# Group softmax on one core: twelve tiles computed in place, stores and loads issued in bursts of six on one DMA ring

## The chip, the cores and the metric

The kernel runs on one core of one Trainium2 chip. The metric is the device time of one execution in microseconds (us); the median of several runs is compared. The engines that matter here are VectorE (DVE in the rows), ScalarE (ACT) and SyncE (SP), which issues all the transfers; 16 DMA engines carry these out. TensorE does nothing, and GpSimd (POOL) only writes four constants.

## The reference

```python
def reference(x):                       # x: 4 x 4096 x 4352, float32
    B, N, D = x.shape
    G = 8
    Dg = D // G                         # 544
    x_g = x.reshape(B, N, G, Dg)
    x_g = x_g - x_g.max(axis=-1, keepdims=True)
    exp = np.exp(x_g)
    out = exp / exp.sum(axis=-1, keepdims=True)
    return out.reshape(B, N, D)
```

Each of the 16,384 rows has 8 groups of 544 numbers, and each group gets its own softmax. The input is read once and the output, which is as large, is written once.

## The kernel before

The rows are cut into 128 tiles of 128 rows (one row for each partition of SBUF); a tile is 128 x 4352 float32, 17,408 bytes in each partition and 2,228,224 bytes in all (2176 KB). For each tile:

- SP issues the load of `xt` (L32).
- VectorE takes the negated maximum of the eight groups into `mx` in one instruction (L35).
- ScalarE computes the exponentials of `xt` into a second tile `ot`, one group at a time, with `mx` as the bias; each of the eight instructions also leaves the sum of its group in `sm` (L40).
- VectorE takes the reciprocals `rs` of the eight sums (L49) and multiplies `ot` by them in place, one group at a time (L51).
- SP issues the store of `ot` (L52).

`xt` and `ot` have four buffers each, eight tiles in all. All 256 transfers go through SP's one queue, and SP issues them in order: where an instruction of SP waits, everything behind it in its list waits too. The framework puts in the semaphores, and it chose the order of the instructions on each engine, which is not that of the loop: in the trace four loads go out together behind one store, and three more stores follow them, in a cycle of four tiles.

Of the kernel before, what the change touches and what calls it, by code (L numbers as in the profile page):

```python
# [1 line left out]

# [4 lines left out]


@with_exitstack
def kernel(  # L10
    ctx: ExitStack,
    tc: tile.TileContext,
    x: bass.AP,
    out: bass.AP,
):
    nc = tc.nc
    G = 8
    P = 128
    xf = x.flatten_outer_dims()
    of = out.flatten_outer_dims()  # L20
    N, D = xf.shape
    Dg = D // G
    xg = xf.rearrange("n (g d) -> n g d", g=G)
    og = of.rearrange("n (g d) -> n g d", g=G)
    ntiles = N // P

    pool = ctx.enter_context(tc.tile_pool(name="io", bufs=4))
    small = ctx.enter_context(tc.tile_pool(name="small", bufs=4))

    for t in range(ntiles):  # L30
        xt = pool.tile([P, G, Dg], mybir.dt.float32)
        nc.sync.dma_start(out=xt, in_=xg[t * P:(t + 1) * P])  # L32

        mx = small.tile([P, G], mybir.dt.float32)
        nc.vector.reduce_max(out=mx, in_=xt, axis=mybir.AxisListType.X, negate=True)  # L35

        sm = small.tile([P, G], mybir.dt.float32)
        ot = pool.tile([P, G, Dg], mybir.dt.float32)
        for g in range(G):
            nc.scalar.activation(  # L40
                out=ot[:, g, :],
                in_=xt[:, g, :],
                func=mybir.ActivationFunctionType.Exp,
                bias=mx[:, g:g + 1],
                scale=1.0,
                accum_out=sm[:, g:g + 1],
            )
        rs = small.tile([P, G], mybir.dt.float32)
        nc.vector.reciprocal(out=rs, in_=sm)  # L49
        for g in range(G):  # L50
            nc.vector.tensor_scalar_mul(out=ot[:, g, :], in0=ot[:, g, :], scalar1=rs[:, g:g + 1])  # L51
        nc.sync.dma_start(out=og[t * P:(t + 1) * P], in_=ot)  # L52


# [1 line left out]
_INS = ['x']  # L56
_OUTS = [((4, 4096, 4352), 'float32')]


# [23 lines left out]
```

## Time and profile before

| what | value |
|---|---|
| median of 3 runs | 1601.17 us (1600.88 to 1601.21) |
| span of the profiled execution, first to last instruction | 1599.5 us |
| median less that span | 1.7 us |
| VectorE busy | 1048.2 us |
| ScalarE busy | 760.8 us |
| bytes moved by SP's queue | 570.44 MB |
| share of the 16 DMA engines' span that its packets took | 85.6% |

The profiled execution's own time is its span and what lies around it; the 1.7 us between the median and the span stands for the latter. Busy shares are averages over the span. The share of the DMA engines counts the time of each packet, and can exceed 1 in a short stretch where packets overlap. Times in the rows are us from the span's start unless they are marked ns.

### The profile page before, as it was taken

What the parts mean: (1) busy time and instruction counts of PE and PEld (TensorE: products, weight loads), DVE (VectorE), ACT (ScalarE), POOL (GpSimd) and SP (SyncE); (2) the same over time, 40 slices, a digit from 0 to 9 for tenths busy, and PEclk for the clock granted to TensorE, in tenths of its full rate; (3) what the DMA queues carried; (4) which work ended last, traced back from release to release, by engine and by line L of the source; (5) the groups of instructions that cost most, each with busy time, mean ns of one, the idle gap of its engine ahead of it and who ended that gap; (6) DMA issues with size and microseconds to landing.
All of it is one profiled execution on the core that took longest, in us unless ns stands there. A gap on an engine that the chain in (4) does not pass through costs nothing.

```text
span 1599.5 us, 4255 instructions
## 1 busy us (share of the span) xinstructions
DVE 1048.2 (66%) x1280; ACT 760.8 (48%) x2049; POOL 0.2 (0%) x4
## 2 busy tenths in 40 slices
DVE  7568655587556775567765677656776567765566
ACT  6245444455444554445544355443554435544354
POOL 0000000000000000000000000000000000000000
DMA  8888998888988889888898888998889988898887
GB/s 362 355 341 349 376 383 346 337 349 369 390 348 341 349 355 390 361 337 353 351 383 369 341 349 355 374 378 336 344 359 376 376 342 341 362 375 371 344 340 312
DMA packets 36897, 570.71 MB, mean 357 GB/s; under 512 B 4096, under 2 KB 4096, under 8 KB 4096
## 3 DMA queue, kind: packets, MB, share of 16 engines
q1 hardware_dynamic: 36864, 570.44, 85.6%
q14 instruction: 33, 0.27, 0.0%
HBM read 285.21 MB, written 285.21 MB: 357 GB/s over the span
## 4 chain that ended last, share of the span: by engine, by line
DMA 33%; DVE 27%; ACT 26%; issue 10%; SPq 1%; DVEq 0%; ACTq 0%
DMA xt<-in_x_dram 33%; ACT ot L40 26%; DVE ot L51 18%; DVE mx L35 8%; DVE rs L49 1%; SPq L32 1%; SPq L52 1%; DVEq L78 0%; ACTq L78 0%
## 5 line engine op out<-in xcount | busy, mean ns | idle before, releaser
L40 ACT ACTIVATE ot<-xt,mx 128x544 f32<-128x544 f32 x1024 | 750.7, 734 | 817.8 <-DVE mx L35 667.3
L35 DVE TENSOR_REDUCE mx<-xt 128x8 f32<-128x4352 f32 x128 | 599.5, 4683 | 426.0 <-DMA xt<-in_x_dram 426.0
L51 DVE TENSOR_SCALAR ot<-ot,rs 128x544 f32<-128x544 f32 x1024 | 434.3, 499 | 4.5
L40 ACT ACTIVATION_READ_ACCUMULATOR ot<-xt,mx 128x1 f32 x1024 | 191.4, 187 | 0.0
L49 DVE RECIPROCAL rs<-sm 128x8 f32<-128x8 f32 x128 | 25.5, 199 | 113.3 <-ACT ot L40 113.3
L40 ACT ACT_TABLE_LOAD x1 | 1.3, 1283 | 9.7 <-DMA xt<-in_x_dram 9.7
L67 POOL MEMSET const-uint8-127<- 128x1 uint8 x1 | 0.1, 102 | 0.0
L67 POOL MEMSET const-bfloat16-1.0<- 128x1 bf16 x1 | 0.1, 101 | 0.0
L67 POOL MEMSET const-float32-0.0<- 128x1 f32 x1 | 0.1, 98 | 0.2 <-issue 0.2
L67 POOL MEMSET const-float32-1.0<- 128x1 f32 x1 | 0.1, 98 | 0.0
## 6 DMA issues: line engine op xcount, KB each, us to landing
xt<-in_x_dram SPq DMA_DIRECT2D x128, 2176.0 KB, 17.1
out_dram<-ot SPq DMA_DIRECT2D x128, 2176.0 KB, 6.6
```

The source lines that it names most:

```text
L32: nc.sync.dma_start(out=xt, in_=xg[t * P:(t + 1) * P])
L35: nc.vector.reduce_max(out=mx, in_=xt, axis=mybir.AxisListType.X, negate=True)
L40: nc.scalar.activation(out=ot[:, g, :], in_=xt[:, g, :], func=mybir.ActivationFunctionType.Exp, bias=mx[:, g:g + 1], scale=1.0, accum_out= ...
L49: nc.vector.reciprocal(out=rs, in_=sm)
L51: nc.vector.tensor_scalar_mul(out=ot[:, g, :], in0=ot[:, g, :], scalar1=rs[:, g:g + 1])
L52: nc.sync.dma_start(out=og[t * P:(t + 1) * P], in_=ot)
L67: nc = _bacc.Bacc("TRN2", target_bir_lowering=False, num_devices=1)
```

## The change

A tile now has one buffer instead of two: ScalarE writes the exponentials over `xt`, VectorE scales them there, and the store reads the same buffer. The pool has twelve buffers instead of eight. The instructions of each engine run in the order in which the program writes them (`manual_schedule`). VectorE's order is the maximum of tile i, then the reciprocals and the scaling of tile i-1. SP's order is twelve loads, then six stores, six loads, six stores, and so on. Load i+12 writes the buffer of tile i, and so it has to wait until store i has landed. Behind the first twelve there are 20 bursts of loads: 19 of six, and one of two. All transfers still go through SP's one queue, and the number and shapes of the instructions on VectorE and ScalarE are the same.

```diff
+    NBUF = 12
...
-    pool = ctx.enter_context(tc.tile_pool(name="io", bufs=4))
+    pool = ctx.enter_context(tc.tile_pool(name="io", bufs=NBUF))
...
-    for t in range(ntiles):
-        xt = pool.tile([P, G, Dg], mybir.dt.float32)
-        nc.sync.dma_start(out=xt, in_=xg[t * P:(t + 1) * P])
+    def load(i):
+        xt = pool.tile([P, G, Dg], f32, name="xt")
+        tiles[i] = xt
+        nc.sync.dma_start(out=xt, in_=xg[i * P:(i + 1) * P])
 
-        mx = small.tile([P, G], mybir.dt.float32)
+    def store(i, eng):
+        eng.dma_start(out=og[i * P:(i + 1) * P], in_=tiles.pop(i))
+
+    def expo(i):
+        xt = tiles[i]
+        mx = small.tile([P, G], f32, name="mx")
         nc.vector.reduce_max(out=mx, in_=xt, axis=mybir.AxisListType.X, negate=True)
-
-        sm = small.tile([P, G], mybir.dt.float32)
-        ot = pool.tile([P, G, Dg], mybir.dt.float32)
+        sm = small.tile([P, G], f32, name="sm")
+        sums[i] = sm
         for g in range(G):
             nc.scalar.activation(
-                out=ot[:, g, :],
+                out=xt[:, g, :],
                 in_=xt[:, g, :],
...
-        rs = small.tile([P, G], mybir.dt.float32)
-        nc.vector.reciprocal(out=rs, in_=sm)
+    def scale(i):
+        xt = tiles[i]
+        rs = small.tile([P, G], f32, name="rs")
+        nc.vector.reciprocal(out=rs, in_=sums.pop(i))
         for g in range(G):
-            nc.vector.tensor_scalar_mul(out=ot[:, g, :], in0=ot[:, g, :], scalar1=rs[:, g:g + 1])
-        nc.sync.dma_start(out=og[t * P:(t + 1) * P], in_=ot)
+            nc.vector.tensor_scalar_mul(out=xt[:, g, :], in0=xt[:, g, :], scalar1=rs[:, g:g + 1])
...
+    B = NBUF // 2
+    with tc.manual_schedule():
+        for i in range(NBUF):
+            load(i)
+        for i in range(nt + 1):
+            if i < nt:
+                expo(i)
+            if i:
+                scale(i - 1)
+                store(i - 1, nc.sync)
+                if i % B == 0:
+                    for j in range(i - B + NBUF, min(i + NBUF, nt)):
+                        load(j)
```

## Rows read from the trace of the kernel before

**Rows 1.** The page: span, busy time of each engine, transfers and their queue

```profile
span 1599.5 us, 4255 instructions
...
DVE 1048.2 (66%) x1280; ACT 760.8 (48%) x2049; POOL 0.2 (0%) x4
...
DMA packets 36897, 570.71 MB, mean 357 GB/s; under 512 B 4096, under 2 KB 4096, under 8 KB 4096
...
q1 hardware_dynamic: 36864, 570.44, 85.6%
```

**Rows 2.** Waits: us in total, times, longest; the engines, whole span

```profile
ACT ot L40 <- DVE mx L35: 667.3, 33, 21.6
DVE mx L35 <- DMA xt<-in_x_dram: 426.0, 64, 13.2
```

**Rows 3.** Waits of SP's own queue, whole span, same columns

```profile
SPq L52 <- DVE ot L51: 1397.0, 127, 24.1
```

**Rows 4.** SP's timeline, two stretches, merged: start, us until the last one's end, count

```profile
0.73 2.80 SPq L32 DMA_DIRECT2D xt<-in_x_dram  x4
...
85.73 22.77 SPq L52 DMA_DIRECT2D out_dram<-ot  x4
108.59 3.96 SPq L32 DMA_DIRECT2D xt<-in_x_dram  x4
```

**Rows 5.** Windows of one cycle: stretch, us, busy (x), clock, DMA share, GB/s

```profile
85.73:91.96 6.23, 6.19 (x6) 3.74 (x11) 0.00 (x0) 1.00 0.85 359
91.96:94.70 2.74, 2.74 (x6) 2.74 (x8) 0.00 (x0) 1.00 0.00 0
94.70:100.08 5.38, 5.34 (x6) 3.21 (x11) 0.00 (x0) 1.00 0.98 414
100.08:102.84 2.76, 1.89 (x5) 2.76 (x9) 0.00 (x0) 1.00 0.01 6
...
108.19:108.97 0.78, 0.00 (x0) 0.00 (x0) 0.00 (x0) 1.00 0.00 0
108.97:115.41 6.44, 0.00 (x0) 0.00 (x0) 0.00 (x0) 1.00 1.04 384
```

**Rows 6.** Windows in which transfers stand back to back, same columns

```profile
37.46:53.26 15.80, 10.85 (x17) 7.46 (x22) 0.00 (x0) 1.00 0.99 422
4.00:22.00 18.00, 10.94 (x7) 8.88 (x22) 0.00 (x0) 1.00 1.00 428
108.97:136.19 27.22, 13.71 (x12) 10.37 (x29) 0.00 (x0) 1.00 0.99 410
```

**Rows 7.** VectorE's timeline, first reduction and one cycle: start, us, idle before

```profile
9.69 4.68 DVE L35 TENSOR_REDUCE mx<-xt 128x8 f32<-128x4352 f32 x1 [9.69 <-DMA xt<-in_x_dram]
...
121.05 4.69 DVE L35 TENSOR_REDUCE mx<-xt 128x8 f32<-128x4352 f32 x1 [12.91 <-DMA xt<-in_x_dram]
126.24 4.69 DVE L35 TENSOR_REDUCE mx<-xt 128x8 f32<-128x4352 f32 x1 [0.51 <-DMA xt<-in_x_dram]
...
135.36 4.68 DVE L35 TENSOR_REDUCE mx<-xt 128x8 f32<-128x4352 f32 x1
...
143.49 4.68 DVE L35 TENSOR_REDUCE mx<-xt 128x8 f32<-128x4352 f32 x1
```

**Rows 8.** The page's costliest groups: busy, mean ns, idle before and releaser

```profile
L40 ACT ACTIVATE ot<-xt,mx 128x544 f32<-128x544 f32 x1024 | 750.7, 734 | 817.8 <-DVE mx L35 667.3
L35 DVE TENSOR_REDUCE mx<-xt 128x8 f32<-128x4352 f32 x128 | 599.5, 4683 | 426.0 <-DMA xt<-in_x_dram 426.0
L51 DVE TENSOR_SCALAR ot<-ot,rs 128x544 f32<-128x544 f32 x1024 | 434.3, 499 | 4.5
```

**Rows 9.** The store's instructions: ns min, median, max; first and last start

```profile
L52 SPq DMA_DIRECT2D out_dram<-ot x128: 332/343/348, 24.1 to 1592.1; - x128
```

**Rows 10.** The page's DMA issues: count, KB each, median us to landing

```profile
xt<-in_x_dram SPq DMA_DIRECT2D x128, 2176.0 KB, 17.1
out_dram<-ot SPq DMA_DIRECT2D x128, 2176.0 KB, 6.6
```

More of the change, by code (lines that the diff above doesn't have):

```diff
@@ L24 @@
     og = of.rearrange("n (g d) -> n g d", g=G)
-    ntiles = N // P
-    pool = ctx.enter_context(tc.tile_pool(name="io", bufs=4))
+    nt = N // P
+    pool = ctx.enter_context(tc.tile_pool(name="io", bufs=NBUF))
     small = ctx.enter_context(tc.tile_pool(name="small", bufs=4))
-    for t in range(ntiles):
-        xt = pool.tile([P, G, Dg], mybir.dt.float32)
-        nc.sync.dma_start(out=xt, in_=xg[t * P:(t + 1) * P])
-        mx = small.tile([P, G], mybir.dt.float32)
+    f32 = mybir.dt.float32
+    tiles = {}
+    sums = {}
+    def load(i):
[7 more added lines that the diff above has]
+        mx = small.tile([P, G], f32, name="mx")
         nc.vector.reduce_max(out=mx, in_=xt, axis=mybir.AxisListType.X, negate=True)
-        sm = small.tile([P, G], mybir.dt.float32)
-        ot = pool.tile([P, G, Dg], mybir.dt.float32)
+        sm = small.tile([P, G], f32, name="sm")
+        sums[i] = sm
         for g in range(G):
             nc.scalar.activation(
-                out=ot[:, g, :],
+                out=xt[:, g, :],
                 in_=xt[:, g, :],
```

## The prediction

> **What bounds the kernel now.** I read the page's totals first. No compute engine fills the span: VectorE is busy for 1048.2 us of 1599.5, ScalarE for 760.8, and the packets of SP's queue for 85.6% of the 16 DMA engines' time [rows 1]. So the transfers are nearest to being the bound, but they too have some 14% over, about 230 us, and the question is who leaves the DMA engines empty, and whether they could go faster when they are not.
>
> The waits answer the first half. ScalarE waits 667.3 us for the maximum, VectorE 426.0 us in 64 waits for loads [rows 2]; and SP, from which the loads must come, stood 1397.0 us in 127 waits for the scaling that a store needs [rows 3]. That is a circle: compute waits for a load, the load stands behind a store in SP's list, the store waits for compute. SP's timeline shows it: four stores at VectorE's pace within 22.77 us, and only behind the last of them four loads in one go [rows 4]. The windows of that cycle show the price: nothing moves for 2.74, 2.76 and 0.78 us, always between one store's end and the next one's start [rows 5]. At these places the engines are not slow, they have nothing queued. VectorE in turn stands idle for 12.91 us, because all four tiles are used up when the loads start [rows 7].
>
> The second half is the rate while something is queued. Loads alone run at 428 GB/s in an 18 us window, and three stores in a row at 422 GB/s, with a DMA share of 1.00 and 0.99 [rows 6]. The mean of 357 GB/s [rows 1] is thus a full rate with holes in it.
>
> **The change, part by part.** The number and shapes of the compute instructions stay, so their busy time stays as in [rows 8], and no byte is saved. What changes is when transfers are queued.
>
> *In place.* VectorE's scaling is in place already, at 499 ns an instruction [rows 8]. For ScalarE writing over what it reads the trace has no row. The bounds: nothing, or the instruction twice as long. ScalarE needs 8 x 0.734 = 5.9 us a tile, and two transfers of a tile take over 10 us (below), so even 11.7 us would only just bind; I take nothing, since the same engine reads and writes as much as before. What hides compute altogether is the transfers: 10.4 us a tile against VectorE's 8.13 us, the distance from one reduction to the next in an undisturbed stretch (143.49 - 135.36) [rows 7].
>
> *Twelve buffers and bursts of six.* Is anything ever missing in the ring? I go through SP's new list. The twelve loads land by 9.69 + 11 x 5.2 = 67 us. Store 0 can be issued at about 24.1 us, as before [rows 9], and store k some 8.13k us later, store 5 at 65 us; the ring gets to them from 67 us on, one every 5.2 us, so all are ready. Load 12 waits for store 0 to land (72 us), load 17 for store 5 (about 99 us); when SP stands at that last wait, loads 12 to 16 are still in the ring, 26 us of work. Stores 6 to 11 stand behind load 17 in SP's list; their data are ready between 73 and 114 us, and the ring reaches them from 130 us on. From then on a cycle of six tiles takes the ring some 63.5 us and VectorE 6 x 8.13 = 48.8 us, so compute catches up with the loads and then follows each as it lands. The added wait is that scaling of tile i-1 stands behind the maximum of tile i on VectorE, and so behind load i. The worst case is the last tile of a burst, whose scaling needs the first load of the next burst; but in the ring that load comes ahead of all six stores of which this is the last, by about 50 us. Issuing costs SP about 1 us a load (3.96 us for four [rows 4]) against 5.2 us of transfer. So I find no hole after the start. At the end the last loads stand ahead of the last eight stores, 42 us, in which two tiles are computed.
>
> *What a transfer costs in a full ring.* A single store takes 5.38 us from its first to its last packet; three back to back take 15.80 us, so each further one costs (15.80 - 5.38) / 2 = 5.21 us [rows 5, 6]. A store with loads right behind it takes 6.44 us instead of 5.38 [rows 5]; this switch from store to load, 1.06 us, is paid once a cycle before and after. From its start to the end of the four loads are 27.22 us, so a load costs (27.22 - 6.44) / 4 = 5.20 us [rows 5, 6]. A switch from load to store shows no price: the store issued at 85.73 us, while the last load was still moving, ended 6.23 us after its issue, and one issued to idle engines lands after 6.6 us [rows 5, 10]. Its bounds are nothing and another 1.06 us; I take nothing.
>
> **The sum.** First load landed at 9.69 us [rows 7]; 127 further loads, 127 x 5.20 = 660.4; 128 stores, 128 x 5.21 = 666.9; 20 switches (20 bursts of loads behind stores), 20 x 1.06 = 21.2; and the end. The last store is issued at 1592.1 of 1599.5 [rows 1, 9], 7.4 us before the end, of which 6.2 are its start and data, so 1.2 us lie behind the data. Together 1359.4 us of span, and with the 1.7 us by which the median exceeds the span, 1361 us: 15% less than 1601.17.
>
> **A rule that speaks against it.** The mean of the whole span is 357 GB/s [rows 1]. The Trainium skill, "DMA: Bandwidth & Descriptors", section "Where 436 GB/s comes from", says that transfers between HBM and SBUF are bound by HBM at about 358 GB/s for a core. By that the kernel stands at its limit already; by the rows it does not, as windows of 14 to 18 us run at 422 to 428 GB/s and the holes hold no packets [rows 5, 6]. The skill's "HBM Reference", section "Specifications (TRN2)", itself adds that a core streaming alone gets well above that share, about 425 GB/s, which is what these rows show.
>
> **The rivals.**
>
> *A ceiling on long stretches.* The rates above come from stretches under 30 us, each with a hole near it. If memory gave 357 GB/s over any longer time, 570.44 MB would need 1598 us, and with start and end about 1600 to 1605: no change. For it speaks only that the mean is near a round share; against it, that each hole ends when compute releases a store [rows 3].
>
> *Slower because reads and writes disturb each other all the time.* Before, loads and stores stand in the ring together only about one store in four, and there the store takes 6.44 us [rows 5]. After, both kinds are queued nearly always. If every transfer then cost 6.44 us, 256 x 6.44 = 1649 us, with 9 us of start, end and surroundings about 1658 us: slower by 3.5%. It decides from a mean of (1601 - 9) / 256 = 6.2 us a transfer. Against it: the four loads behind that store pay nothing, though all are queued at once.
>
> *A lower sustained rate.* If back-to-back transfers fell to the 5.38 us of a single store, 256 x 5.38 = 1377, plus 21.2 and 7 for start, end and surroundings: 1406 us.
>
> *The ring runs dry once a cycle*, say at the wait of the sixth load for the sixth store, by a hole like those of 2.74 us [rows 5]: 20 x 2.74 = 55 us, 1416 us; several such holes, up to 1590. Against it stand the 26 us in the ring at that moment.
>
> *The switch costs less or more.* If it is free in long bursts, 1340 us; if load to store costs 1.06 us as well, 1382 us.
>
> **Numbers.** The full ring, with the switch at any of its bounds (1338 to 1383): 0.78. Less than that: 0.02. The lower sustained rate (1384 to 1410): 0.08. A dry ring (to 1590): 0.06. The ceiling: 0.03. Slower through disturbance: 0.03. The range 1338 to 1400 us takes in the first and most of the lower rate, and leaves out under 2 in 10. A difference of 0.2% is about what a measurement of this kernel can tell from none: faster 0.94, within it 0.03, slower 0.03.
>
> **What would show it.** Right: SP's queue has packets for over 95% of the span, windows of 50 us in its middle show 410 to 425 GB/s, and no window of 2 us is empty between the start and the end; VectorE's only large wait is for loads, about 300 us in all (1359 less 1048); SP's waits are for landed stores rather than for the scaling. Wrong: empty windows at each change of bursts (dry ring), a share near 1 at 360 GB/s (ceiling or disturbance, which differ in whether stores or all packets are longer), ScalarE's exponentials well over 734 ns (in place), or VectorE busy without a break.

## The result, and the profile after

The changed kernel takes 1342.9 us (median of 4 runs, 1342.61 to 1343.89) against 1601.15 us: a ratio of 0.8389, 95% interval 0.8377 to 0.8401, faster by 16.1%. 1361 us was forecast, 1338 to 1400 as the range. The direction and the mechanism were right, the time lies 18 us under the forecast.

The page of the changed kernel answers to [rows 1], [rows 8] and [rows 10]; its line numbers are those of the new code (L45 maximum, L49 exponentials, L63 scaling, L37 load, L40 store):

```profile
span 1342.1 us, 4119 instructions
...
DVE 1038.4 (77%) x1280; ACT 764.4 (57%) x2049; POOL 0.2 (0%) x4
...
GB/s 400 427 430 427 432 430 432 427 431 429 431 429 430 431 431 430 431 431 430 431 430 431 430 431 431 430 430 431 431 431 430 430 431 429 431 430 432 431 430 258
...
q1 hardware_dynamic: 36864, 570.44, 99.4%
...
L49 ACT ACTIVATE xt<-xt,mx 128x544 f32<-128x544 f32 x1024 | 751.3, 735 | 539.5 <-DVE mx L45 295.5
L45 DVE TENSOR_REDUCE mx<-xt 128x8 f32<-128x4352 f32 x128 | 599.0, 4679 | 270.7 <-DMA xt<-in_x_dram 270.7
...
xt<-in_x_dram SPq DMA_DIRECT2D x128, 2176.0 KB, 31.1
out_dram<-xt SPq DMA_DIRECT2D x128, 2176.0 KB, 41.3
```

The compute engines work as long as before, on a shorter span: 1038.4 and 764.4 us. The same 570.44 MB fill 99.4% of the DMA engines' time where they filled 85.6%, and the rate is 427 to 432 GB/s in all slices but the first and the last; the last falls to 258.

SP's own waits answer to [rows 3] (us in total, times, longest):

```profile
SPq L37 <- DMA out_dram<-xt: 715.4, 116, 15.1
SPq L40 <- DMA xt<-in_x_dram: 371.7, 81, 5.8
SPq L37 <- DMA xt<-in_x_dram: 66.0, 14, 5.0
SPq L40 <- DVE xt L63: 42.3, 6, 13.4
```

The 1397.0 us of waiting for the scaling are down to 42.3. What SP now waits for is landed transfers, loads too, which the program's data would not ask for. The ring holds the transfers that have been issued and have not landed. The stores' median from issue to landing says how many these are when a store goes out: 41.3 us is eight transfers of 5.17 us (below). SP never has more than eight in flight in this trace; the ninth load goes out at 9.35 us, when the first has landed. That wait was not foreseen, and it costs nothing, because seven are left in the ring.

The windows of the middle and of the end answer to [rows 6]; columns as there, the DMA share is the last but one:

```profile
100.00:1300.00 1200.00, 935.09 (x1154) 686.53 (x1843) 0.00 (x0) 1.00 1.01 430
600.00:650.00 50.00, 43.72 (x51) 29.82 (x80) 0.00 (x0) 1.00 1.00 429
1000.00:1050.00 50.00, 35.73 (x44) 24.97 (x67) 0.00 (x0) 1.00 1.01 433
...
1322.00:1324.00 2.00, 0.00 (x0) 0.00 (x0) 0.00 (x0) 1.00 1.01 435
1326.00:1334.00 8.00, 0.00 (x0) 0.00 (x0) 0.00 (x0) 1.00 0.26 111
1336.00:1340.00 4.00, 0.00 (x0) 0.00 (x0) 0.00 (x0) 1.00 0.12 52
```

At 431 GB/s, the mean of the two windows of 50 us, a transfer of 2,228,224 bytes takes 2.228 / 0.431 = 5.17 us. The end shows something new: from 1326 us on the share is 0.26 and then 0.12, that is four and then two of the 16 DMA engines. Twelve are done at about 1326 us, and the last two work 15 us longer.

This does not arise at the end. A transfer lands in 16 parts, and the trace keeps the time of each. The last part came 1.8 us after the first for a transfer that landed at 114 us, 10.0 us after it at 675 us and 15.6 us at the end; at 345 us four parts were already 3.0 to 5.8 us behind. So the lag builds up over the whole span, by about 1%. Which engines these are, and why they are slower, the trace does not show.

### The profile page after: what moved, and what is told of

Read it like the earlier page. It is cut to its first block, busy times and chain, and to the rows that moved or that the text cites. A ratio compares the mean times of both kernels' runs of the same rounds, so it can differ in the third digit from the quotient of the medians.

```text
span 1342.1 us, 4119 instructions
## 1 busy us (share of the span) xinstructions
DVE 1038.4 (77%) x1280; ACT 764.4 (57%) x2049; POOL 0.2 (0%) x4
## 3 DMA queue, kind: packets, MB, share of 16 engines
q1 hardware_dynamic: 36864, 570.44, 99.4%
## 4 chain that ended last, share of the span: by engine, by line
DMA 92%; DVE 4%; ACT 1%; issue 1%; SPq 0%; DVEq 0%; ACTq 0%
DMA out_dram<-xt 61%; DMA xt<-in_x_dram 31%; DVE mx L45 2%; DVE xt L63 2%; ACT xt L49 1%; SPq L40 0%; SPq L37 0%; DVE rs L61 0%; DVEq L105 0%; ACTq L105 0%
## 5 line engine op out<-in xcount | busy, mean ns | idle before, releaser
L49 ACT ACTIVATE xt<-xt,mx 128x544 f32<-128x544 f32 x1024 | 751.3, 735 | 539.5 <-DVE mx L45 295.5
L45 DVE TENSOR_REDUCE mx<-xt 128x8 f32<-128x4352 f32 x128 | 599.0, 4679 | 270.7 <-DMA xt<-in_x_dram 270.7
L63 DVE TENSOR_SCALAR xt<-xt,rs 128x544 f32<-128x544 f32 x1024 | 434.2, 498 | 4.5
L49 ACT ACTIVATION_READ_ACCUMULATOR xt<-xt,mx 128x1 f32 x1024 | 191.5, 187 | 0.0
## 6 DMA issues: line engine op xcount, KB each, us to landing
out_dram<-xt SPq DMA_DIRECT2D x128, 2176.0 KB, 41.3
```

The source lines that it names most:

```text
L49: nc.scalar.activation(out=xt[:, g, :], in_=xt[:, g, :], func=mybir.ActivationFunctionType.Exp, bias=mx[:, g:g + 1], scale=1.0, accum_out= ...
L63: nc.vector.tensor_scalar_mul(out=xt[:, g, :], in0=xt[:, g, :], scalar1=rs[:, g:g + 1])
```

## The experiments

Two questions were put: which part of the change the gain comes from, and what became of the 1.06 us that a change from store to load was to cost. All times below are medians; ratios are to the kernel before, run on the same chip.

**alt1: one store and one load in turn.**

```diff
-    B = NBUF // 2
+    B = 1
+    AHEAD = 7
+    nxt = NBUF
...
-                    for j in range(i - B + NBUF, min(i + NBUF, nt)):
-                        load(j)
+                    while nxt < min(i + AHEAD, nt):
+                        load(nxt)
+                        nxt += 1
```

> The changed kernel with one store and one load in turn instead of bursts of six (loads run six to seven tiles ahead of the stores): 116 changes from store to load instead of 20, and the ring as full as before. In the changed kernel 12 of the 16 DMA engines end at about 1325.5 us and four end 15 us later. Theory A, each change from store to load costs a few of the engines about 0.77 us (15.4 / 20), and the slowest sets the end: 1343 + 96 x 0.77 = about 1417 us. Rival B, those four engines are simply slower per byte, whatever the order: no change, 1343 us. Rival C, the price of the prediction, 1.06 us on all engines for each change: 1343 + 96 x 1.06 = about 1445 us.

1342.42 us, ratio 0.8386 (0.8372 to 0.8400): no change. Theories A and C are out: 96 more changes of direction cost nothing. The bursts of six bring nothing by themselves. Two windows of this kernel, the middle and the end:

```profile
600.00:650.00 50.00, 38.58 (x47) 28.77 (x78) 0.00 (x0) 1.00 1.01 431
...
1326.00:1330.00 4.00, 0.00 (x0) 0.00 (x0) 0.00 (x0) 1.00 0.25 109
```

The full rate, and at the end again four engines that are late. That agrees with rival B, as does the lag that grows over the whole span in the changed kernel; why these engines are slower no run shows.

**burst11: bursts of eleven.** As alt1, with `B = 11` and `AHEAD = 12`.

> The changed kernel with bursts of eleven stores and eleven loads instead of six: 11 changes from store to load instead of 20. Theory A (0.77 us each on the slowest engines): 1343 - 9 x 0.77 = about 1336 us. Rival B (four engines slower per byte): 1343 us. Rival D, the longer bursts leave the ring empty because scaling of a burst's last tile waits for a load far behind in the list: above 1350 us, with windows in which nothing moves.

1339.61 us (1339.44 to 1339.66), ratio 0.8367 (0.8355 to 0.8380): the fastest of all kernels run here, 3 us under alt1 on the same chip. It is not theory A's saving, which alt1 ruled out. Its end looks different:

```profile
1326.00:1330.00 4.00, 3.51 (x9) 0.00 (x0) 0.00 (x0) 1.00 0.84 357
1330.00:1335.00 5.00, 0.00 (x0) 0.00 (x0) 0.00 (x0) 1.00 0.97 411
```

VectorE still works on the last tile until almost 1330 us, and the last store then runs on nearly all 16 engines at once. Here the end is set by compute, in the changed kernel and alt1 by the late engines. Those lag less here: for the transfers that land after 1300 us the last part comes 9.2 us behind the first at the median, against 15.6 us in the changed kernel. Why they do, and so where the 3 us come from, is not shown.

**inplace12: the buffers alone.** The loop of the kernel before, in its own order:

```diff
-    pool = ctx.enter_context(tc.tile_pool(name="io", bufs=4))
+    pool = ctx.enter_context(tc.tile_pool(name="io", bufs=12))
...
-        ot = pool.tile([P, G, Dg], mybir.dt.float32)
...
-                out=ot[:, g, :],
+                out=xt[:, g, :],
```

> The kernel before with the first half of the change alone: computed in place in a pool of twelve tiles, the order of instructions left to the framework, which still puts a store at VectorE's pace ahead of each burst of four loads. Theory, the order of SP's list makes the time and the buffers do not: 1600 us, no change from before. Rival, the buffers alone let loads run ahead: 1343 to 1400 us.

1600.47 us, ratio 0.9997 (0.9987 to 1.0006). In place and twelve tiles, and nothing gained: the framework's order still has a store at VectorE's pace ahead of each four loads, as in [rows 4].

```profile
85.51 22.77 SPq L51 DMA_DIRECT2D out_dram<-xt  x4
108.33 3.99 SPq L32 DMA_DIRECT2D xt<-in_x_dram  x4
```

**order8: the order alone, with the eight tiles of before.** The changed kernel with `NBUF = 4`, a second tile `ot` in the pool for the output, and so two stores and two loads in turn.

```diff
-    NBUF = 12
+    NBUF = 4
...
+        ot = pool.tile([P, G, Dg], f32, name="ot")
...
-                out=xt[:, g, :],
+                out=ot[:, g, :],
```

> The second half of the change alone: the eight tiles of the kernel before (four for the input, four for the output, not in place), the order written out, two stores and two loads in turn on SP's queue, 62 changes from store to load. Theory, the order alone takes nearly all of the gain: 1343 to 1376 us (with theory A's 0.77 us for each of 42 more changes 1375). Rival, without twelve buffers the ring runs dry in each cycle: above 1450 us.

1449.70 us, ratio 0.9059 (0.9039 to 0.9080): more than half of the gain, and 107 us short of the change. The theory missed. The rival's number (above 1450 us) is met within the spread of the runs (1447.0 to 1455.2), but not its reason, as the page shows. Behind it stand the spread of the stores' times to landing, windows of three transfers in a row, and one of four cycles:

```profile
span 1445.2 us, 4255 instructions
...
q1 hardware_dynamic: 36864, 570.44, 99.2%
...
xt<-in_x_dram SPq DMA_DIRECT2D x128, 2176.0 KB, 16.3
out_dram<-ot SPq DMA_DIRECT2D x128, 2176.0 KB, 9.4
...
DMA to landing us min/median/max: 6.6/9.4/18.8
```

```profile
702.00:707.85 5.85, 5.82 (x9) 3.68 (x11) 0.00 (x0) 1.00 1.01 384
707.85:713.00 5.15, 0.91 (x3) 3.42 (x10) 0.00 (x0) 1.00 1.01 433
713.00:719.50 6.50, 4.66 (x2) 0.00 (x0) 0.00 (x0) 1.00 1.00 345
...
702.00:791.00 89.00, 63.82 (x81) 46.38 (x125) 0.00 (x0) 1.00 1.00 395
```

Apart from one hole of 2.7 us at 30 us, and the last stores, the ring does not run dry: its packets fill 99.2% of the span. They take longer. In these rows a store, a load and a second load follow one another. The load with another load behind it runs at 433 GB/s; the store ahead of the change to loads runs at 384 and the load ahead of the change to stores at 345, which is 0.7 and 1.3 us more. Over 49 cycles in the middle of the trace, taken from landing to landing (the median of a transfer's 16 parts), a store ahead of loads takes 5.9 us and a load ahead of stores 6.2, the other two 5.2. That is 1.7 us more a cycle, and 62 cycles make 105 us of the 107 that are missing. This is a price like that of [rows 5], paid at both kinds of change, in a kernel without holes; alt1 changes direction almost twice as often and pays nothing. What differs is how much stands in the ring. The median of 9.4 us stands between two groups, as the stores of a pair go out in different states of the ring: one half land about 9 us after their issue, the other about 18. The times from issue to landing of all transfers, added up and divided by the span, give the mean number in flight: 2.7 here, 7.8 in alt1.

**alt_d4 and alt_d2: the alternating kernel with fewer transfers in flight.** As alt1, with `AHEAD = 10` and `AHEAD = 11`: a load waits for a later store.

> The alternating kernel (one store, one load in turn, twelve tiles in place), with the loads three tiles further ahead, so that each load has to wait for the landing of the store three before it and SP never has more than about five transfers in flight, where it had eight (a transfer then took 41.4 us from issue to landing, eight times 5.17). Nothing else changes; two to four transfers are still queued at every moment, so no hole. Theory E, a change of direction in the ring costs time when few transfers stand in the ring and none when it is deep: with about 1 us for each of the 232 changes of direction, 1450 to 1580 us. Rival F, the price has to do with stores that go out right behind compute, or with the tile addresses in the two-tile order, not with the depth: 1342 us, no change.

1341.44 us, ratio 0.8379 (0.8367 to 0.8392): no price. The medians to landing were 25.8 and 30.5 us, five to six transfers. Theory E asked for few transfers in the ring, and this may not have been few enough; the next run goes lower.

> As the run before it, one tile further: each load waits for the landing of the store two before it, so that about three transfers are in flight. Theory E: at least as slow as the kernel with about five in flight, 1450 to 1620 us, packets of over 1 us in every transfer, share of the queue above 95%. Rival F: 1342 us. Rival G, what is lost is lost to holes at the waits: 1400 us or more, with empty windows and a share below 90%.

1368.31 us (1357.98 to 1373.88), ratio 0.8539 (0.8502 to 0.8577), with medians to landing of 15.7 and 20.8 us, three to four transfers. Neither theory's number; the rate over the 40 slices of its span (34 us each) and four windows say why:

```profile
GB/s 400 427 426 430 430 432 431 431 430 432 431 431 432 431 432 430 432 431 421 406 393 404 405 404 395 387 407 412 400 428 413 432 430 430 431 431 422 386 428 324
```

```profile
500.00:600.00 100.00, 79.84 (x96) 55.49 (x151) 0.00 (x0) 1.00 1.01 431
650.00:750.00 100.00, 73.71 (x91) 53.66 (x144) 0.00 (x0) 1.00 1.00 402
750.00:850.00 100.00, 72.92 (x91) 53.66 (x144) 0.00 (x0) 1.00 1.00 400
1050.00:1150.00 100.00, 78.66 (x96) 58.09 (x157) 0.00 (x0) 1.00 1.01 431
```

In the profiled execution the same turns run at the full 431 GB/s for 600 us, then at about 400 for some 400 us, then at the full rate again, and once more slowly near the end. At this depth the price comes and goes, with no hole (rival G is out). So the price hangs on the state of the ring, not on the order of the list.

The slow slices are those in which the late engines are farthest behind. From 100 us on, every slice in which the last part of a transfer lands less than 7.5 us after the first runs at 427 GB/s or more; in every slice under 415 the lag is 8.1 to 9.1 us. It had grown to that by 650 us, fell to 7 by 1060 and came back to 8 at about 1230. A lag of 8 us is one and a half transfers, so that of the 3.7 in flight on average about two would be left for the engines that are ahead. That is an estimate, and that it is the reason was not tested.

**n8, n6, n4: the changed kernel with fewer tiles.** `NBUF = 8`, `6` and `4`, bursts of half as many.

> The changed kernel with eight tiles instead of twelve, as much memory as before, and so bursts of four stores and four loads (30 changes from store to load). The fourth load of a burst waits for the landing of the store just ahead of the burst, with three loads left in the ring at that moment. Theory E, with 1.7 us a cycle as in the kernel with the order alone (105 us over 62 cycles): 1343 to 1394 us, by how often the ring is shallow at a change. Rival, in place and a written-out order are all that counts and the ring is deep enough: 1343 us. Rival, eight tiles leave the ring dry: above 1400 us with empty windows.

1341.53 us, ratio 0.8378 (0.8364 to 0.8392). With the memory of the kernel before, in place: all of the gain.

> The changed kernel with six tiles, bursts of three: three quarters of the memory of the kernel before. The third load of a burst waits for the landing of the store just ahead of the burst, with two loads left in the ring. If two or three queued transfers are enough, 1342 us as with eight and twelve tiles; if the shallow ring costs what it cost in the kernel with the order alone (1.7 us a cycle, 42 cycles), about 1413 us.

1342.20 us, ratio 0.8383 (0.8371 to 0.8396); medians to landing 15.5 and 20.3 us. Three quarters of the memory of before, and still all of the gain.

> The changed kernel with four tiles, bursts of two: half the memory of the kernel before. By hand the ring has one load left at each wait for a store, and the second store of a pair is scaled only shortly before the ring comes to it. No hole and no price: 1345 us. The price of the kernel with the order alone (1.7 us a cycle, 63 cycles): about 1450 us. A hole of 2.7 us at each of 63 pairs as well: about 1620 us, no better than before.

1436.91 us, ratio 0.8979 (0.8966 to 0.8993). A full queue, but nearly the price of order8:

```profile
span 1434.5 us, 4135 instructions
...
q1 hardware_dynamic: 36864, 570.44, 99.4%
...
xt<-in_x_dram SPq DMA_DIRECT2D x128, 2176.0 KB, 11.3
out_dram<-xt SPq DMA_DIRECT2D x128, 2176.0 KB, 9.5
```

Again half of the stores land within two transfers' time; on average 2.1 transfers are in flight, in n6 3.5 and in n8 4.8.

**sep12: order8 with six input and six output tiles.** `NBUF = 6`, `B = 2`.

> The kernel with the order alone (not in place, two stores and two loads in turn), with six input and six output tiles instead of four and four: the same instructions and the same turns, 61 cycles, only the loads run two tiles further ahead. Theory, what it lacked was depth in the ring, so that stores at VectorE's pace left only two or three transfers queued: 1340 to 1360 us. Rival, the loss of 107 us came from not computing in place or from turns of two: 1440 to 1455 us.

1340.91 us, ratio 0.8376 (0.8363 to 0.8388). The 107 us that order8 lacked are back without computing in place and with turns of two: it lacked depth in the ring (6.2 in flight on average against 2.7). SP waits 128 times for the scaling here too (last line), so that stores which go out right behind compute are not the cause; that was the first half of rival F.

```profile
xt<-in_x_dram SPq DMA_DIRECT2D x128, 2176.0 KB, 33.3
out_dram<-ot SPq DMA_DIRECT2D x128, 2176.0 KB, 28.6
...
SPq L41 <- DVE ot L67: 1147.8, 128, 19.4
```

**perm8: order8 with the tiles taken in another order**, `(i * 37) % nt` for `i` in the load and in the store.

> The kernel with the order alone and its eight tiles, but the tiles of the input and the output are taken in another order (tile i of the list is tile 37 i mod 128 in memory), so that the load and the store that stand next to each other in the ring are 17 tiles or more apart in memory instead of three. The result is the same. Theory K, the packets of over 1 us come from the distance of the two addresses: 1343 to 1400 us. Rival, from the state of the ring: 1445 to 1455 us, no change.

1452.68 us, ratio 0.9078 (0.9063 to 0.9094). That the load and the store next to each other are only three tiles apart in memory is not the cause; at 17 tiles or more the price is the same. Other relations of the addresses were not tried.

**two_rings: the stores from ScalarE's queue.**

```diff
-                store(i - 1, nc.sync)
+                store(i - 1, nc.scalar)
```

> The changed kernel with the stores issued by ScalarE's queue instead of SP's: loads and stores then stand in two rings and the DMA engines take from both. Theory, the 16 DMA engines are the bound and take the same 5.17 us a transfer from either ring: 1335 to 1350 us. Rival, reads and writes mixed packet by packet pay the price of the change of direction all the time: above 1450 us.

1342.89 us, ratio 0.8388 (0.8375 to 0.8400): one ring or two makes no difference. The Trainium skill, "DMA: Bandwidth & Descriptors", section "Issuing engines are not separate DMA queues", says that transfers run on the same 16 engines whichever engine issued them; this run agrees.

## Why the prediction was right, and where its sizes were off

*The bound.* Right. The 14% that the transfers had over were holes which SP's list made, and the change filled them: inplace12 keeps the list and gains nothing, every kernel with a list that runs ahead gains 9 to 16%.

*The ring never dry.* Right: no window of the middle has a hole, the windows of 50 us show 429 to 433 GB/s where 410 to 425 was said, and VectorE's only large wait is for loads, 270.7 us where about 300 was said. SP's waits were said to be for landed stores; they are for landed transfers of both kinds, by the limit of eight.

*In place at no cost.* Right: the exponentials take 735 ns against 734 [rows 8].

*The sum.* Against the 1359.4 us of span forecast, 1342.1:

| term | forecast | measured |
|---|---|---|
| first load landed | 9.69 | 9.35 |
| 255 further transfers | 660.4 + 666.9 = 1327.3 | 255 x 5.17 = 1318.4 |
| 20 changes from store to load | 21.2 | none that shows: 5.18 for a store ahead of loads |
| behind that, to the end | 1.2 | 14.4 (1342.1 less the two terms above) |

Three terms were mis-sized. The pitch, 5.20 and 5.21 us, came from stretches of three or four transfers that began at an idle ring; 50 us of full ring give 5.17 for the mix, 9 us less in all. From landing to landing a load behind a load takes 5.19 us and a store behind a store 5.14, so it is mainly the store that was put too high. And the 1.06 us for a change of direction [rows 5] was taken for a price of the change itself. In the kernels run here it is paid where few transfers are in flight: alt1 pays nothing for 116 of them, order8 pays at most of its changes, alt_d2 for some 400 us of its span, there for loads ahead of a store alone (5.4 us at the mean, 5.2 for the stores). The kernel before had an empty ring ahead of the store in question [rows 5], so its trace could show the price only in that state; behind that store four loads were queued, so whether it is the same price is not shown.

The third is the end: 14.4 us where 1.2 was said, as the prediction did not have the late engines. So about 13 of the 21 us come back in another place. That is luck: without them the time would be about 1330 us (1342.9 less 13.2, an estimate), under the 1338 at which the range begins. The 1340 us that the prediction gave for a free switch comes nearest, by the same luck.

*The rivals.* The ceiling of 357 GB/s is out: 430 GB/s hold for over 1200 us, half reads and half writes. So the rule of the Trainium skill that the HBM side binds at about 358 ("DMA: Bandwidth & Descriptors", section "Where 436 GB/s comes from") does not hold for this one core, and the measurement decides; the sentence in "HBM Reference", section "Specifications (TRN2)", on a core streaming alone (about 425 GB/s) is borne out. (The windows that the prediction calls 14 to 18 us long are 15.80 and 18.00 us long in [rows 6].) The lower sustained rate and the dry ring did not come. Reads and writes that disturb each other did not come in the changed kernel. The longer transfers of order8 and n4 look like this rival, at 7 to 8% of the rate, not enough to be slower than before; that disturbance is their cause is not shown.

*What stays open.* Why a change of direction costs time in a shallow ring and not in a deep one. The runs exclude the number of changes (alt1), computing in place (n4 has the price in place, sep12 has none out of place), stores right behind compute (sep12), a distance of only three tiles between the addresses (perm8) and holes (shares of 99%). What orders the kernels is the mean number in flight. At 2.1 (n4) and 2.7 (order8, perm8) the price is paid all through the span; at 3.5 (n6) it does not show in the time, and at 3.7 (alt_d2) it is paid in part; from 4.8 on (n8, alt_d4 and all others) it is gone. The kernel before, with 2.1, pays at the change to loads alone. That n6 is free with fewer in flight than alt_d2 says that the mean is not the whole of it. What the DMA engines do differently there, and why some of them are slower, no trace here shows.

## What to carry to other kernels

A mean rate below the rate of the busy stretches points at the list of the queue first, as here, and not at memory: look at what the issuing engine waits for, and at which transfers stand behind that wait. Let loads run so far ahead that four or more transfers are in flight; with three to four one kernel here was free and one lost 2%. Six tiles in place, eight in place or six and six all reach within 3 us of the best, and more buffers, longer bursts or a second ring add at most those 3 us. A full queue is not yet a fast one: order8 and n4 have shares of 99% and lose 7 to 8% in longer packets, and the times from issue to landing show that the ring is shallow. Add them up and divide by the span; a median can stand between two groups.

## What the runs showed of the hardware that was not expected

- A change between loads and stores costs time where few transfers are in flight: 0.7 us on the transfer ahead of the change to loads and 1.0 on the one ahead of the change to stores with 2.7 in flight (order8, over 49 cycles), nothing that shows with 7.8 (alt1).
- It can come and go within one execution: 431 GB/s, then 400 to 402, then 431 with the same instructions (alt_d2). The slow slices are those in which the last part of a transfer lands 8 to 9 us after the first.
- One core moved 430 GB/s for over 1200 us, reads and writes alike.
- The parts of a transfer drift apart in a long full ring: the last of 16 lands 1.8 us after the first at 114 us and 15.6 us after it at the end of the changed kernel, and four engines still work when the others are done.
